# One decoding and prompt step of a hybrid network: the decays' exponents bounded on ScalarE instead of VectorE

## The chip, the cores and the metric

The kernel runs on 1 core of one Trainium2 chip. Its time is the device time of one execution in microseconds (us), the median of several runs. Engines are named as in the profile: PE (TensorE matmul), PEld (TensorE weight load), DVE (VectorE), ACT (ScalarE), POOL (GpSimd), SP (SyncE, which issues the DMAs here). Each engine works through its own list of instructions in order: an instruction that waits holds up all that stand behind it on that engine.

## What is computed

Two layers over 512 prompt tokens and 8 decode tokens, width 1024, all in float32. Layer 0 mixes with a gated DeltaNet (GDN, 8 heads), layer 1 with a Mamba-2 state space scan (SSD, 32 heads in 4 groups); after each mixer comes a LayerNorm, a gated convolutional feed-forward network and a second LayerNorm. The change touches one piece of each mixer, the decay matrix inside a chunk:

```python
gcum = jnp.cumsum(gc, axis=2)                       # GDN: running sum of the log decays, never rising
gamma = jnp.exp(jnp.where(incl, gcum_h[..., :, None] - gcum_h[..., None, :], -jnp.inf))
qk = jnp.einsum('bnihd,bnjhd->bnhij', qc, kc) * gamma
...
seg = jnp.exp(jnp.where(incl, acum_h[..., :, None] - acum_h[..., None, :], -jnp.inf))   # SSD
cb = jnp.einsum('bnigs,bnjgs->bngij', cc, bc)
scores = seg.reshape(...) * cb[:, :, :, None]       # one mask-and-decay product for each head
y_diag = jnp.einsum('bnghij,bnjghp->bnighp', scores, xg)
```

Where i is before j the difference is positive and its exponential could overflow. The kernel bounds the exponent at zero and masks the product afterwards (the mask is already in `CB`, and in GDN a later product with `U` does it).

## The kernel before

Tokens lie along the free axis in two halves of 260 columns, features on the 128 partitions, and a chunk is 128 tokens (C = 4 chunks). `plan` writes a list of units; one unit is one output tile of 128 rows of one weight matrix, for one or both halves of the tokens. `unit` (L225) issues, for each half and each 128 rows of the contraction, three matmuls (L243: high parts, and the two cross products of high and low parts of weights and x), so 24 matmuls for a half unit with a contraction of 1024. `prep` loads a unit's weights (512 KB), rounds them on ACT (L220) and makes the low part on DVE or POOL (L221). `unit_bank` gives the accumulators: two PSUM banks, and outside the GDN's scan a third. A bank is free again when ACT has copied it out, in GDN by L590 (`u<-psl`), in SSD by L425 and L439 (`u<-psl`) or by the gate's L1035 (`z<-psl`).

A tile `u` then goes through a short convolution (`conv`: one ACT instruction at L413, three DVE instructions at L416) and a Silu on ACT (L601 in GDN, L1052 in SSD).

The GDN layer asks for the decays of a head in `gdn_decays` (L727): one DMA spreads the head's running sums over all partitions (`gbc<-gd`), four DVE instructions add the column of the token j and bound at zero (L734, one for each chunk, 128x128), one ACT instruction takes the exponential of the whole tile (L736).

The SSD layer calls `ssd_group` for each of the 4 groups when the group's last x tile is through its convolution. After the product `CB` of C and B (L1143), the transposed x times dt (`xdt`, L1157) and the chunk states (matmul `sst` L1164; `Sn`, L1167 to L1170), it goes over 4 pairs of heads. Each head loads `E` by one DMA (`sE<-ad`, L1181), bounds it by four DVE instructions (L1183, in order `(E - a) min 0`), takes the exponential on ACT (L1185), multiplies by `CB` (L1187: on DVE for the second head of a pair, on POOL for the first), and PE uses it (`yd`, L1189). `yo` (L1193) brings in the states. The decode tokens' work (L1233 to L1246) and the D term (L1200) are on DVE beside it.

The code is written in the order of the computation, but the order on each engine is set by a scheduler that places every instruction by its own estimates of durations (`schedule_with_timeline_sim=True`); `high_priority()` marks what it should place early. A change in one instruction's engine can so move others anywhere in the program. ACT needs one table set for Exp, another for Silu and another for Sqrt; where neighbours on ACT differ, the compiler puts a table load (`ACT_TABLE_LOAD`) between them.

Of the kernel before, what the change touches and what calls it, by code (L numbers as in the profile page):

```python
# [13 lines left out]
ALU = mybir.AluOpType  # L14
# [8 lines left out]
B = 8  # L23
# [50 lines left out]
class Net:  # L74
# [39 lines left out]
    def unit_bank(self):  # L114
        """Two banks, and outside the GDN's scan a third."""
# [13 lines left out]
    def plan(self):  # L129
        """units: (name, m, halves, [(chunk, first block in it, first k, number of k)]) in order of use;  # L130
        chunks: (array, index, first block, number of blocks), the weights that are loaded together."""
# [42 lines left out]
    def _parts(self, name, nm, ka, kb, nfull):  # L174
        """Rows 0 .. nm first over k < ka (tag a), then over the rest (b), the other rows at once."""
# [25 lines left out]
    def lo_pool(self, i):  # L201
        """Whether the low parts of a unit's weights are made on GpSimd."""
        name, _, halves, _ = self.units[i]
        return name in ("gin", "sin") and len(halves) == 2 and (name == "gin" or i % 4 != 3)
# [20 lines left out]
    def unit(self, evac):  # L225
        """Runs the next unit; evac(name, m, half, psum)."""
# [66 lines left out]
    def ln_add(self, xr, out, m, h, ps):  # L293
        """The residual plus the first products."""
# [3 lines left out]
    def ln_evac(self, name, m, h, ps):  # L298
        """Rows of x, less the mean of the first NS of them."""
# [64 lines left out]
    def ln_half(self, h, row):  # L364
# [4 lines left out]
        # d = x - shift, whose sum over the first rows is 0: the variance is mean(d^2) - mean(d)^2  # L369
# [50 lines left out]
    def first_half(self, w, key, ps, keep):  # L420
        """The first half of a tile that a convolution takes: kept, or in DRAM until the second is there."""
# [89 lines left out]
    def softplus(self, pool, z, n, tag):  # L511
        """max(z, 0) + log1p(exp(-|z|)), the logarithm as 2 atanh(e / (2 + e))."""
# [17 lines left out]
    def rsqrt_small(self, pool, x, y, n, tag):  # L530
        """y = x ** -0.5 for a few columns: the exponent's half as the start, then Newton's steps."""
# [9 lines left out]
    def rsqrt(self, out, ps, eps):  # L541
        """out = (ps + eps) ** -0.5"""
# [5 lines left out]
    def tokens(self, pool, raw, name):  # L548
        """[64, T] -> [P, C + 1, 64], tokens on partitions; the last block holds the decode tokens."""
# [892 lines left out]
```

## Time and profile before

| | us |
|---|---|
| median of 3 runs | 1802.03 |
| lowest and highest run | 1801.03, 1809.23 |
| span of the profiled execution (first to last instruction) | 1799.5 |
| PE busy | 1613.9 (90%) |
| DVE busy | 1256.9 (70%) |
| POOL busy | 938.5 (52%) |
| ACT busy | 836.7 (46%) |

The page gives no other time for the profiled execution than its span. The span is 2.5 us under the median and 1.5 us under the lowest run; that much lies around the span. The shares are averages over stages that differ: the GDN's heads run from about 48 to 408 us, the SSD's groups from about 948 to 1228 us, and the feed-forward networks fill most of the rest. A PE that shows busy is not a PE at its peak, since matmuls are pipelined.

### The profile page before, as it was taken

How to read it: one execution, taken by the hardware profiler on the slowest of the kernel's cores; microseconds unless marked ns; L12 is line 12 of the kernel's file. 1: busy time of each engine (PE TensorE's matmuls, PEld its weight loads, DVE VectorE, ACT ScalarE, POOL GpSimd, SP SyncE). 2: the span in 40 equal slices, each digit the busy share in tenths (PEclk: the TensorE clock that was granted, in tenths of full speed). 3: DMA queues.
4: the chain of work that ended last, by engine and by line, in shares of the span. 5: the costliest groups of instructions: out<-in, count | busy, mean ns of one | idle time of the engine just before them, and what ended most of it. 6: DMA issues, size and time to landing. Idle time of an engine off the chain costs nothing.

```text
span 1799.5 us, 33950 instructions
## 1 busy us (share of the span) xinstructions
PE 1613.9 (90%) x12889; PEld 1550.6 (86%) x12889; DVE 1256.9 (70%) x2379; ACT 836.7 (46%) x1724; POOL 938.5 (52%) x1058
## 2 busy tenths in 40 slices
PE   7789888888899899999988888989989998899996
PEld 7788887788799899999887787879988998889996
DVE  5977897977876554336779988885659756554356
ACT  4554554335564344214665564645336633343134
POOL 4654555634538741225345757666224387876252
PEclk9999999899999999999999999999999999999998
DMA  5421333234466533334545434342464665664334
GB/s 181 135 84 60 95 112 104 86 110 155 135 200 213 177 121 97 88 98 122 163 148 172 150 124 140 118 136 65 146 197 150 203 205 174 196 213 153 95 101 143
DMA packets 108980, 250.38 MB, mean 139 GB/s; under 512 B 15344, under 2 KB 31696, under 8 KB 108784
## 3 DMA queue, kind: packets, MB, share of 16 engines
q1 hardware_dynamic: 108816, 248.20, 44.0%
q8 instruction: 101, 1.65, 0.4%
q14 instruction: 63, 0.52, 0.1%
HBM read 225.80 MB, written 22.92 MB: 138 GB/s over the span
## 4 chain that ended last, share of the span: by engine, by line
PE 32%; DVE 26%; DMA 17%; POOL 13%; ACT 6%; issue 5%; SPq 1%; ACTq 0%; DVEq 0%; POOLq 0%
PE psl L243 27%; DVE lo L221 4%; DMA Sr<-bd 3%; POOL Sd L993 3%; DMA raw<-w_up 3%; DVE sE L1183 3%; POOL Sr L991 2%; ACT hi L220 2%; DVE y L416 2%; POOL fl L276 2%; DMA raw<-w_down 2%; POOL Sd L992 2%; DMA Sr<-kr 2%; DMA Sd<-sstate 1%; DVE Xtmp L815 1%
## 5 line engine op out<-in xcount | busy, mean ns | idle before, releaser
L243 PE MATMUL psl<-XH,hi 128*128 128x260 f32 (+1 forms) x2816 | 818.9, 292 | 57.2 <-ACT u L439 18.7
L243 PE MATMUL psl<-XL,hi 128*128 128x260 f32 (+1 forms) x2848 | 823.4, 290 | 9.3 <-DVE lR L305 3.1
L243 PE MATMUL psl<-XH,lo 128*128 128x260 f32 (+1 forms) x2816 | 811.7, 289 | 4.3 <-DVE lo L221 3.9
L243 PEld LDWEIGHTS psl<-XH,hi 128*128 128x128 f32 (+1 forms) x2816 | 539.4, 192 | 72.7 <-ACT u L439 22.2
L221 DVE TENSOR_TENSOR lo<-raw,hi 128x512 fp32r<-128x512 f32 (+2 forms) x439 | 360.2, 856 | 321.4 <-ACT hi L220 313.7
L243 PEld LDWEIGHTS psl<-XL,hi 128*128 128x128 f32 (+1 forms) x2848 | 546.0, 192 | 16.6 <-issue 5.9
L243 PEld LDWEIGHTS psl<-XH,lo 128*128 128x128 f32 (+1 forms) x2816 | 539.5, 192 | 10.9 <-DVE lo L221 7.1
L220 ACT CAST hi<-raw 128x512 fp32r<-128x512 f32 (+2 forms) x499 | 314.2, 669 | 445.8 <-PE psl L243 209.0
L243 PE MATMUL psl<-fh,lo 128*128 128x260 f32 x704 | 201.5, 286 | 1.4 <-DVE lo L221 1.0
L243 PE MATMUL psl<-fh,hi 128*128 128x260 f32 x704 | 200.6, 285 | 0.0
L243 PE MATMUL psl<-fl,hi 128*128 128x260 f32 x704 | 199.0, 283 | 0.0
L221 POOL TENSOR_TENSOR lo<-raw,hi 128x1024 fp32r<-128x1024 f32 x60 | 147.5, 2458 | 62.2 <-ACT hi L220 60.7
L243 PEld LDWEIGHTS psl<-fh,lo 128*128 128x128 f32 x704 | 132.8, 189 | 3.3 <-DVE lo L221 3.0
L243 PEld LDWEIGHTS psl<-fh,hi 128*128 128x128 f32 x704 | 132.9, 189 | 0.5
L243 PEld LDWEIGHTS psl<-fl,hi 128*128 128x128 f32 x704 | 132.7, 189 | 0.3
L276 POOL TENSOR_TENSOR fl<-f,fh 128x260 fp32r<-128x260 f32 x88 | 79.9, 910 | 64.8 <-ACT fh L275 64.8
L416 DVE SCALAR_TENSOR_TENSOR s<-u,par,s 128x512 f32<-128x512 f32 x88 | 90.1, 1023 | 9.3 <-ACT s L413 8.1
L275 ACT CAST fh<-f 128x260 fp32r<-128x260 f32 x88 | 35.8, 407 | 91.3 <-DVE f L478 91.3
L243 PE MATMUL psl<-y,hi 128*128 128x260 f32 x256 | 73.3, 288 | 1.8 <-DVE y L276 0.8
L993 POOL TENSOR_TENSOR Sd<-Sd,Sr 128x512 f32<-128x512 f32 x48 | 69.4, 1445 | 0.6
L362 POOL TENSOR_TENSOR lnsq<-lnsq,sq 128x260 f32<-128x260 f32 x48 | 48.3, 1009 | 28.9 <-ACT sq L360 27.4
L1183 DVE TENSOR_SCALAR sE<-sE,acum 128x128 f32<-128x128 f32 x128 | 59.6, 525 | 3.0 <-DMA sE<-ad 2.9
(404 smaller groups left out, 2656.8 us busy)
## 6 DMA issues: line engine op xcount, KB each, us to landing
raw<-w_up SPq DMA_DIRECT2D x106, 512.0 KB
raw<-w_down SPq DMA_DIRECT2D x44, 512.0 KB
raw<-w_sin SPq DMA_DIRECT2D x43, 512.0 KB
raw<-w_gin SPq DMA_DIRECT2D x32, 512.0 KB
Sd<-sstate SPq DMA_DIRECT2D x64, 256.0 KB
raw<-w_down SPq DMA_DIRECT2D x22, 384.0 KB
Sd<-gstate SPq DMA_DIRECT2D x32, 256.0 KB
kb<-kr SPq DMA_DIRECT2D x32, 256.0 KB
```

The source lines that it names most:

```text
L220: nc.scalar.copy(out=hi[:, ks, :mw], in_=raw[:, ks, :])
L221: eng.tensor_tensor(out=lo[:, ks, :mw], in0=raw[:, ks, :], in1=hi[:, ks, :mw].bitcast(F32), op=ALU.subtract)
L243: self.nc.tensor.matmul(out=ps[h][:mw], lhsT=w[:, b0 + k, :mw], rhs=x[:, hs], start=(k0 + k == first and i == 0), stop=(k0 + k == last and ...
L275: nc.scalar.copy(out=hi, in_=xf)
L276: (eng or nc.gpsimd).tensor_tensor(out=lo, in0=xf, in1=hi.bitcast(F32), op=ALU.subtract)
L362: nc.gpsimd.tensor_tensor(out=acc, in0=acc, in1=sq, op=ALU.add)
L416: nc.vector.scalar_tensor_tensor(out=y[:, :S], in0=u[:, j:j + S], scalar=self.pcol(wname, i * w + j), in1=y[:, :S], op0=ALU.mult, op1=ALU.add)
L815: nc.vector.tensor_tensor(out=tmp[:, :, :, i:], in0=_bc(X16[:, None, :, i:], [P, 2, C, n]), in1=D[:, i:i + 2, :, i:], op=ALU.mult)
L991: nc.gpsimd.tensor_tensor(out=t, in0=t, in1=_bc(col[:, :, None], D4), op=ALU.mult)
L992: nc.gpsimd.tensor_tensor(out=St, in0=St, in1=_bc(decay[:, :, None], D4), op=ALU.mult)
L993: nc.gpsimd.tensor_tensor(out=St, in0=St, in1=t, op=ALU.add)
L1183: nc.vector.tensor_scalar(out=E[:, c, :], in0=E[:, c, :], scalar1=self.acum[:, c, h:h + 1], scalar2=0.0, op0=ALU.subtract, op1=ALU.min)
```

## The change

The bound becomes a rectifier on ACT, which takes the column of token j as its bias: `Relu(G_i' + G_j)` in GDN, where the loaded row is already negated, and `Relu(-E + a)` in SSD. The exponential that follows then has the scale -1. In SSD, the product with `CB` is on DVE for both heads of a pair. The diff also drops the comments and one line, so that line numbers behind L734 are smaller by one in the changed kernel, and by three behind L1187.

```diff
     def gdn_decays(self, p, h):
...
         for c in range(C):
-            nc.vector.tensor_scalar(out=gbc[:, c, :], in0=qe[:, c, :], scalar1=self.gcum[:, c, h:h + 1], scalar2=0.0,
-                                    op0=ALU.add, op1=ALU.max)
+            nc.scalar.activation(out=gbc[:, c, :], in_=qe[:, c, :], func=AF.Relu, bias=self.gcum[:, c, h:h + 1])
         nc.scalar.activation(out=both, in_=both, func=AF.Exp, scale=-1.0)
...
     def ssd_group(self, p, g, Bt, Ct):
...
                 for c in range(C):
-                    nc.vector.tensor_scalar(out=E[:, c, :], in0=E[:, c, :], scalar1=self.acum[:, c, h:h + 1], scalar2=0.0,
-                                            op0=ALU.subtract, op1=ALU.min)
-                nc.scalar.activation(out=E, in_=E, func=AF.Exp)
-                eng = nc.vector if s else nc.gpsimd
-                eng.tensor_tensor(out=E, in0=E, in1=CB, op=ALU.mult)
+                    nc.scalar.activation(out=E[:, c, :], in_=E[:, c, :], func=AF.Relu, scale=-1.0, bias=self.acum[:, c, h:h + 1])
+                nc.scalar.activation(out=E, in_=E, func=AF.Exp, scale=-1.0)
+                nc.vector.tensor_tensor(out=E, in0=E, in1=CB, op=ALU.mult)
```

The instructions counted: 32 in GDN (8 heads, 4 chunks) and 128 in SSD (32 heads, 4 chunks) go from DVE to ACT, and 16 products go from POOL to DVE. Over the whole program ACT has 70 table loads before and 72 after: 15 and 19 of them before the GDN layer's end, 43 and 41 among the SSD groups. None of the loads stands before a rectifier.

The order on the engines, at the places of which the prediction speaks. First DVE in the SSD layer, around the copy `Sn<-sst` that starts the states of the second group; `sE` is the decay tile, `dy` and `Sd` belong to the decode tokens. Before:

```order
L1241 TENSOR_REDUCE dy<-Sd 128x4
L1187 TENSOR_TENSOR sE<-sE,CB 128x512
L1246 SCALAR_TENSOR_TENSOR y<-y,par,dy 128x8
L221 TENSOR_TENSOR lo<-raw,hi 128x1024
L1183 TENSOR_SCALAR sE<-sE,acum 128x128 x8
L1170 COPY Sn<-sst 128x512
L1241 TENSOR_REDUCE dy<-Sd 128x4
```

And now:

```order
L1243 SCALAR_TENSOR_TENSOR y<-y,par,dy 128x8
L1184 TENSOR_TENSOR sE<-sE,CB 128x512
L1241 TENSOR_TENSOR dyt<-xdd,bcd 128x8
L1197 SCALAR_TENSOR_TENSOR y<-y,par,yd 128x512
L1184 TENSOR_TENSOR sE<-sE,CB 128x512
L1238 TENSOR_REDUCE dy<-Sd 128x4
L1169 COPY Sn<-sst 128x512
```

The eight bounds ahead of the copy are gone, and products with `CB` stand there.

Next ACT at the first SSD group, from the first bounds on; `u<-psl` are the copies that free a bank. Before, the stretch from the copy of the tile behind the group's C:

```order
L220 CAST hi<-raw 128x1024
L439 COPY u<-psl 128x260
L1185 ACTIVATE sE<-sE 128x512
L1148 COPY Bk<-bt 128x512
L413 ACTIVATE y<-u,par 128x520
L1185 ACTIVATE sE<-sE 128x512
L1052 ACT_TABLE_LOAD
L1052 ACTIVATE C<-C 128x520
L425 COPY u<-psl 128x260
```

And now:

```order
L1182 ACTIVATE sE<-sE,acum 128x128 x8
L1183 ACTIVATE sE<-sE 128x512
L220 CAST hi<-raw 128x1024
L439 COPY u<-psl 128x260
L1147 COPY Bk<-bt 128x512
L1183 ACTIVATE sE<-sE 128x512
L1182 ACTIVATE sE<-sE,acum 128x128 x4
L1051 ACT_TABLE_LOAD
L1051 ACTIVATE C<-C 128x520
L1182 ACTIVATE sE<-sE,acum 128x128 x4
L413 ACTIVATE y<-u,par 128x520
L425 COPY u<-psl 128x260
```

Eight rectifiers now stand ahead of the first of the two copies and eight more between them.

Last ACT at the start of the GDN's heads, from one copy `u<-psl` (L590) on. Before:

```order
L590 COPY u<-psl 128x260
L413 ACTIVATE kq<-u,par 128x520
L590 COPY u<-psl 128x260
L736 ACTIVATE gbc<-gbc 128x1024 x2
L220 CAST hi<-raw 128x1024
L590 COPY u<-psl 128x260
L601 ACT_TABLE_LOAD
L601 ACTIVATE kq<-kq 128x520 x2
L413 ACTIVATE kq<-u,par 128x520
L590 COPY u<-psl 128x260
```

And now:

```order
L734 ACTIVATE gbc<-gbc,gc 128x128 x8
L413 ACTIVATE kq<-u,par 128x520
L590 COPY u<-psl 128x260
L735 ACTIVATE gbc<-gbc 128x1024
L734 ACTIVATE gbc<-gbc,gc 128x128 x2
L601 ACT_TABLE_LOAD
L601 ACTIVATE kq<-kq 128x520
L734 ACTIVATE gbc<-gbc,gc 128x128 x2
L735 ACT_TABLE_LOAD
L735 ACTIVATE gbc<-gbc 128x1024
L734 ACTIVATE gbc<-gbc,gc 128x128 x4
L220 CAST hi<-raw 128x1024
```

The list goes on with a table load, `kq<-kq` and `v<-v` at L601, and only then the next copy `u<-psl`; a table load, the exponential at L735, another table load, `kq<-kq` and the copy after that follow. Before, two instructions of exponentials and one cast stand between the second copy and the third; now there are eight rectifiers, two exponentials, three table loads, three Silus and a cast.

## Rows read from the trace of the kernel before

**Rows 1.** The page's first part: each engine's busy time, its share of the span and its instructions.

```profile
PE 1613.9 (90%) x12889; PEld 1550.6 (86%) x12889; DVE 1256.9 (70%) x2379; ACT 836.7 (46%) x1724; POOL 938.5 (52%) x1058
```

**Rows 2.** Busy time of each engine by stretches of the span: the stretch in us, its length, then the busy us (and instructions) of PE, PEld, DVE, ACT and POOL, the granted TensorE clock as a share of the full 2.4 GHz, the DMA share and GB/s. The first stretch holds the GDN's heads, the second the SSD's groups, the others are parts of the second.

```profile
48.00:408.00 360.00, 305.31 (x2574) 290.12 (x2573) 303.01 (x845) 175.94 (x498) 192.43 (x228) 0.93 0.31 96
...
948.00:1228.00 280.00, 242.25 (x1820) 220.95 (x1820) 253.38 (x430) 152.90 (x217) 184.40 (x144) 0.95 0.43 134
960.00:1058.00 98.00, 80.50 (x593) 71.24 (x594) 92.71 (x178) 60.07 (x80) 64.13 (x53) 0.95 0.47 148
...
1100.00:1152.00 52.00, 46.12 (x328) 40.06 (x328) 45.60 (x83) 30.08 (x39) 39.73 (x31) 0.93 0.46 142
...
1196.00:1228.00 32.00, 27.01 (x187) 23.54 (x186) 27.36 (x51) 14.10 (x20) 22.84 (x18) 0.89 0.38 120
```

**Rows 3.** The chain of waits that ended last, within 948 to 1228 us, as shares of that stretch by engine and line.

```profile
by line: DVE sE L1183 16.4%; PE psl L243 9.9%; DVE y L416 8.6%; issue 5.3%; DMA sE<-ad 4.7%; DVE dy L1241 4.1%; DVE sE L1187 3.0%; DVE Sd L1240 2.6%; DVE y L1273 2.5%; DVE C L416 2.5%; PE yd L1189 2.5%; POOL sE L1187 2.0%; POOL lo L221 1.9%
```

**Rows 4.** For whom PE waited within 948 to 1228 us: waiting line, awaited line, us in total, times, longest.

```profile
PE yo L1193 <- DVE Sn L1170: 9.7, 2, 5.7
PE xtk L509 <- DVE xdt L1157: 7.9, 3, 2.9
```

**Rows 5.** Instructions in order of time on DVE and on PE within the SSD's groups: start, us, engine, line, operation, tiles, count; in brackets the idle time before and what ended it.

```profile
959.50 0.86 DVE L1183 TENSOR_SCALAR sE<-sE,acum 128x128 f32<-128x128 f32 x4
...
1007.80 5.25 DVE L1183 TENSOR_SCALAR sE<-sE,acum 128x128 f32<-128x128 f32 x4
...
1016.10 0.60 PE L1193 MATMUL yo<-C,Sn 128*128 128x128 f32 x3 [2.97 <-DVE ea L1201]
...
1036.71 3.47 DVE L1183 TENSOR_SCALAR sE<-sE,acum 128x128 f32<-128x128 f32 x8
...
1040.83 0.80 PE L1193 MATMUL yo<-C,Sn 128*128 128x128 f32 x2 [5.68 <-DVE Sn L1170]
...
1120.80 3.04 DVE L1183 TENSOR_SCALAR sE<-sE,acum 128x128 f32<-128x128 f32 x4
...
1127.57 1.19 PE L1164 MATMUL sst<-xd,Bk 128*128 128x512 f32 x1 [4.27 <-DVE y L1246]
...
1206.90 5.92 DVE L1183 TENSOR_SCALAR sE<-sE,acum 128x128 f32<-128x128 f32 x8
...
1214.79 0.80 PE L1193 MATMUL yo<-C,Sn 128*128 128x128 f32 x2 [4.05 <-DVE Sn L1170]
```

**Rows 6.** POOL's instructions in order of time, in the same columns, while the second run of rows 5 was on DVE.

```profile
1008.09 2.35 POOL L221 TENSOR_TENSOR lo<-raw,hi 128x1024 fp32r<-128x1024 f32 x1
1010.41 1.31 POOL L1038 TENSOR_TENSOR y<-y,z 128x520 f32<-128x520 f32 x1
```

**Rows 7.** Groups of instructions: line, engine, operation, tiles and shapes, count, busy us and mean ns of one, idle time before them. The first two rows are DVE within 948 to 1228 us, the third POOL over the whole span, the fourth DVE within 48 to 408 us.

```profile
L1183 DVE TENSOR_SCALAR sE<-sE,acum 128x128 f32<-128x128 f32 x128 | 59.6, 525 | 3.0 <-DMA sE<-ad 2.9
L1187 DVE TENSOR_TENSOR sE<-sE,CB 128x512 f32<-128x512 f32 x16 | 15.9, 1004 | 2.4 <-ACT sE L1185 2.4
...
L1187 POOL TENSOR_TENSOR sE<-sE,CB 128x512 f32<-128x512 f32 x16 | 24.3, 1526 | 14.0 <-ACT sE L1185 14.0
...
L734 DVE TENSOR_SCALAR gbc<-gbc,gc 128x128 f32<-128x128 f32 x32 | 11.6, 412 | 4.3 <-DMA gbc<-gd 4.3
```

**Rows 8.** Two rows on ACT instructions of the same size that take a column for each partition: the group of L753 over the whole span (busy us, mean ns of one), and two of it back to back in order of time.

```profile
L753 ACT ACTIVATE Kd<-kt,gdec 128x128 f32<-128x128 f32 x32 | 10.5, 395 | 0.0
...
66.72 0.63 ACT L753 ACTIVATE Kd<-kt,gdec 128x128 f32<-128x128 f32 x2
```

**Rows 9.** The bounds of SSD (L1183) by stretches: the stretch, its length, DVE's busy us on them and their count.

```profile
960.00:1058.00 98.00, 37.31 (x78) 0.95 0.47 148
1100.00:1152.00 52.00, 13.94 (x32) 0.93 0.46 142
1196.00:1228.00 32.00, 7.82 (x16) 0.89 0.38 120
```

**Rows 10.** The start of the GDN's heads in order of time: ACT, and one row each of DVE and PE.

```profile
46.91 0.36 ACT L590 COPY u<-psl 128x260 f32<-128x260 f32 x1
47.31 0.82 ACT L413 ACTIVATE kq<-u,par 128x520 f32<-128x520 f32 x1
48.04 0.36 ACT L590 COPY u<-psl 128x260 f32<-128x260 f32 x1
50.19 1.07 ACT L736 ACTIVATE gbc<-gbc 128x1024 f32<-128x1024 f32 x1 [1.79 <-DVE gbc L734]
...
53.34 1.03 ACT L220 CAST hi<-raw 128x1024 fp32r<-128x1024 f32 x1
54.27 0.37 ACT L590 COPY u<-psl 128x260 f32<-128x260 f32 x1
54.66 1.28 ACT L601 ACT_TABLE_LOAD   x1
55.95 1.17 ACT L601 ACTIVATE kq<-kq 128x520 f32<-128x520 f32 x2
...
57.74 0.35 ACT L590 COPY u<-psl 128x260 f32<-128x260 f32 x1
...
48.19 1.96 DVE L734 TENSOR_SCALAR gbc<-gbc,gc 128x128 f32<-128x128 f32 x4 [1.28 <-DMA gbc<-gd]
...
54.69 0.39 PE L243 MATMUL psl<-XH,hi 128*128 128x260 f32 x1 [1.36 <-ACT u L590]
```

## The prediction

> **What bounds the kernel now.** I read the page's first part, then the stretches, then in the stretch that the change touches the chain of waits, PE's waits, and last the instructions in order of time. Over the whole span PE is the busiest engine at 90%, DVE 70%, ACT 46% [rows 1]. That mean hides the SSD's groups, 948 to 1228 us: there DVE is busy 253.4 of 280 us and PE 242.3, and in 960 to 1058 us, where the bounds of two groups fall together, DVE is busy 92.7 of 98 us, PE 80.5 and ACT 60.1 [rows 2]. So in that stretch DVE sets the pace. The chain says the same: the bounds (L1183) hold 16.4% of it, 46 of 280 us, more than any other line [rows 3]. PE's longest waits there end with DVE [rows 4].
>
> In order of time one sees why. Four bounds take 0.86 us where nothing hinders them, and 5.25 us in another place; eight take 3.47 or 5.92 us [rows 5]. During the 5.25 us POOL ran one long elementwise instruction after the other [rows 6]. The mean bound takes 525 ns and all 128 hold DVE for 59.6 us [rows 7]; at the unhindered spacing, 0.86 / 4 = 0.215 us, they would take 27.5 us. More than half of their time is a stall. The Trainium skill ("SBUF — State Buffer", section "Who interferes with whom") says that DVE and GpSimd share a pair of ports, which one of them holds for a whole instruction, and that ACT never waits for it. The trace agrees as to DVE (0.86 against 5.25 us); that a rectifier on ACT stays free of it, no row here shows.
>
> **What goes from DVE in SSD.** All of the 59.6 us, and 16 more products with CB come: 16 x 1.004 = 16.1 us at the mean of those that DVE does now [rows 7]. Net 43.5 us less for DVE in the groups. POOL loses 24.3 us [rows 7], which was not what PE waited for. What of it lies on PE's path: four waits of PE stand directly behind a run of bounds, 2.97 (1016 us), 5.68 (1041 us), 4.27 (1128 us) and 4.05 us (1215 us) [rows 5]. That is 17.0 us, 8.65 of it in the first burst and 8.3 in the later two. I take these as what the change can give; PE's whole idle time there, 280 - 242.3 = 37.7 us [rows 2], is the upper end.
>
> **What comes to ACT.** No row shows a rectifier. The nearest are 128x128 instructions with a column for each partition, 395 ns alone, and 0.63 us for two back to back, so 0.24 us for each one that follows [rows 8]. Bounds: 0.24 and 0.395 us. The order has them in runs of 4 and 8, so I take 0.39 + 7 x 0.24 = 2.07 us for eight, 0.26 each. All 160 are then 41.6 us (38 to 63).
>
> 128 - 32 - 16 = 80 of the SSD's bounds fall in the first burst or just ahead of it [rows 9]. They put 80 x 0.26 = 20.8 us on top of ACT's 60.1 there: 81 of 98 us, 83%, more than ACT holds in any stretch now [rows 2]. On its in-order list the copies that free PE's banks stand behind runs of rectifiers (order of ACT at the first SSD group). Ten runs of eight could each hold a copy by 2.07 us, 20.7 us in all, or none, since PE has three banks there. I take 6 us, nearer to none. So the first burst gives 8.65 - 6 = 2.65 us.
>
> In the later bursts ACT is at 30.1 of 52 and 14.1 of 32 us [rows 2], with room for 32 x 0.26 = 8.3 and 16 x 0.26 = 4.2 us (counts of [rows 9]). The 8.3 us of waits go; but these 48 bounds belong to 6 pairs of heads, so 6 of POOL's products are now on DVE, 6 x 1.004 us, and I put half of them ahead of something that PE waits for (`xdt`, L1157 [rows 4]): 3 us. Together 8.3 - 3 = 5.3 us.
>
> SSD: -2.65 - 5.3 = **-8 us**.
>
> **GDN.** DVE loses 32 bounds, 11.6 us [rows 7], of 303.0 busy us in 360 [rows 2]. The danger is the start, where four heads' decays come at once. I walk ACT's list there (last order fence) with durations of [rows 8, 10]. The first copy ends at 47.27 us. The decays land at 48.19 (the DVE row waited for them until then). Eight rectifiers 2.07, the convolution's 0.73 (it overlaps its follower): the second copy starts at 51.0 instead of 48.04. Then 0.36 + exponential 1.07 + two rectifiers 0.63 + table load 1.28 + Silu 0.64 + two rectifiers 0.63 + table load 1.28 + exponential 1.07 + four rectifiers 1.11 + cast 1.03 + table load 1.28 + two Silus 1.17 = 11.55 us: the third copy at 62.6 instead of 54.27, **8.3 us later**. The fourth: 0.37 + 1.28 + 1.07 + 1.28 + 0.64 = 4.6, at 67.2 instead of 57.74, 9.5 us later. PE has only two banks in this stage and waited 1.36 us for the third copy already [rows 10]; it can't run ahead, and the first head's keys and queries pass through the same list. The four table loads that the order adds in GDN are all in this stretch and counted.
>
> What comes back: the 16 bounds of the later heads leave DVE, 16 x 0.215 (unhindered) to 16 x 0.412 us [rows 7], 3.4 to 6.6 us on an engine that is 84% busy; I take 4. GDN: +8.3 - 4 = **+4 us** (from -4, if the start is absorbed by waits that PE had anyway, to +13, if nothing comes back).
>
> **The sum.** -8 + 4 = -4 on a span of 1799.5, so 1795.5, and 2.5 us around it as the median of the runs has it: **1798 us**. A measurement of this kernel tells about 0.5% (9 us) from no change, so this forecast is "no difference", with a slight lean to faster.
>
> **Rivals.**
>
> *The DVE relief goes through to PE.* If ACT finds room between its waits, and PE gets back the 17.0 us of waits, the 7.9 us for `xdt` [rows 4], and with fewer gaps a granted clock nearer to 1.00 than the 0.95 of this stretch [rows 2] (at half of that, 242 x 0.025 = 6 us), SSD gives 31 us, less some 3 us for the products on DVE: 28. With GDN at +4: 1802 - 24 = **1778 us**. For it: the chain's 46 us and a DVE at 95% in the first burst. Against: ACT at 83% there.
>
> *ACT becomes what the stage waits for (slower).* With 0.395 us for each rectifier the first burst puts 80 x 0.395 = 31.6 us on ACT, 91.7 of 98 us, and ACT still has to wait for data. It decides from the point where ACT's list, work plus waits, is longer than the burst: ACT idles 38 of 98 us now, and if 18 of these remain, the burst takes 91.7 + 18 = 110 us, 12 more. The later bursts keep their 5 us gain, GDN has +13: 1802 + 12 - 5 + 13 = **1822 us**. The Trainium skill ("ScalarE: Activation LUTs", section "Rules for kernel authors") says to do relu, max and min on VectorE and not on ScalarE. By the unhindered row it is right for one instruction, 0.215 us against 0.26 to 0.395; by the mean of 0.525 us it is not. The rule leads to this rival.
>
> *Nothing moves.* Waits of PE go over to other late work of DVE and DMA, GDN's start is absorbed: 1802 us. It would lie with the forecast in the same verdict. That the change adds more table loads than counted (72 against 70 in all) is excluded by the order.
>
> **How the numbers follow.** Forecast (around 1798, own range 1790 to 1808) 0.43; relief passed on (1765 to 1790) 0.30; ACT the bound (1811 to 1826) 0.20; nothing moves 0.07. Faster by over 0.5% (below 1793): the second case and a part of the first, 0.36. Slower (above 1811): the third and a little, 0.21. Within: 0.43. The range from **1773 to 1822** leaves out about 2 in 10: the better half of the second case's lower part and the worst of the third.
>
> **What would show it.** In the changed profile: the bounds on ACT at 0.24 to 0.40 us each; DVE in the SSD's groups down from 253 to about 210 busy us, ACT up from 153 to about 186, PE's waits behind `Sn` (L1169 there) gone. The third copy `u<-psl` of [rows 10] at about 62 us, and PE idle before it by some 8 us with ACT as the releaser. In the first burst ACT above 80% and waits of PE for ACT's copies, which are absent there now. The prediction is wrong if the first SSD burst becomes shorter by more than 8 us, if PE doesn't wait at the GDN's start, or if ACT takes over the chain of the whole SSD stage.

## The result: 1821.2 us, 0.97% slower, and the profile after

The median is 1821.2 us (1816.56 to 1824.54, 5 runs) against 1802.03 us; the ratio is 1.0097, with a 95% interval from 1.0077 to 1.0117. The profiled execution has a span of 1821.0 us, 21.5 more than before. Four views tell where they went. First the page's busy times, which answer to [rows 1]:

```profile
PE 1631.9 (90%) x12889; PEld 1566.7 (86%) x12889; DVE 1206.8 (66%) x2235; ACT 888.0 (49%) x1886; POOL 912.2 (50%) x1042
```

DVE has 50 us less, ACT 51 more, as meant. But PE, whose work is the same to the instruction, is busy for 18 us longer.

Second, the stretches. They are cut at the same piece of work in both kernels: the first runs from half unit 9 of the projection matmuls (L243, 24 matmuls each) to half unit 96, which is the GDN heads and the LayerNorm behind them; the second runs from the first `cb` matmul of SSD to the last `yo`. Columns as in [rows 2]. Before:

```profile
40.38:513.56 473.18, 405.10 (x3341) 384.52 (x3339) 390.69 (x1019) 241.81 (x636) 237.68 (x287) 0.95 0.36 110
948.91:1241.73 292.82, 255.95 (x1932) 234.62 (x1933) 257.15 (x435) 156.47 (x224) 197.40 (x152) 0.95 0.43 133
```

With the change, and behind them three bursts that answer roughly, not instruction by instruction, to the last three of [rows 2]:

```profile
40.47:539.45 498.98, 422.39 (x3341) 400.56 (x3340) 383.73 (x987) 256.93 (x672) 237.60 (x286) 0.91 0.34 105
973.25:1257.74 284.49, 255.00 (x1911) 233.79 (x1912) 216.94 (x322) 191.71 (x349) 171.77 (x136) 0.96 0.43 137
975.00:1070.00 95.00, 84.02 (x601) 73.67 (x601) 79.96 (x128) 78.24 (x155) 52.59 (x46) 0.95 0.52 168
1115.00:1170.00 55.00, 48.00 (x366) 43.36 (x365) 39.27 (x58) 37.13 (x72) 39.32 (x29) 0.97 0.48 152
1212.00:1244.00 32.00, 26.20 (x173) 22.29 (x172) 29.16 (x41) 20.77 (x37) 24.93 (x18) 0.89 0.42 128
```

The SSD groups are 8.3 us shorter (292.82 to 284.49). Here they are cut once more, at the last `yd` matmul of the second group, two rows before and two with the change:

```profile
948.91:1050.87 101.96, 82.66 (x614) 73.44 (x614) 99.25 (x189) 61.80 (x82) 68.23 (x55) 0.95 0.48 152
1050.87:1241.73 190.86, 173.29 (x1319) 161.18 (x1319) 157.90 (x247) 94.67 (x144) 129.16 (x97) 0.96 0.40 122
...
973.25:1062.18 88.93, 77.95 (x554) 68.09 (x554) 77.98 (x127) 72.24 (x142) 52.02 (x44) 0.94 0.53 169
1062.18:1257.74 195.56, 177.04 (x1359) 165.71 (x1359) 138.96 (x195) 119.46 (x208) 119.76 (x92) 0.97 0.39 122
```

PE's idle time falls from 19.3 to 11.0 us in the first two groups, and rises from 17.6 to 18.5 in the last two. PE has 60 instructions fewer in the first part and 40 more in the second (some records are missing from a trace).

The GDN stretch is 25.8 us longer: PE's idle time grew from 68.1 to 76.6 us, 8.5, and its busy time from 405.1 to 422.4, 17.3, for the same 3341 instructions. The granted clock explains the latter in this pair: 405.1 x 0.95 / 0.91 = 422.9. But the split between waits and clock belongs to the pair. The kernels e2, e5, e6 and e15 below leave the GDN layer as it was, with the same order on PE, ACT, DVE and POOL, and their profiled executions, on several chips, show other splits of nearly the same length. Those of e5 and e15:

```profile
40.40:516.43 476.03, 413.42 (x3340) 393.70 (x3339) 390.61 (x1019) 241.85 (x636) 237.33 (x287) 0.92 0.36 110
...
40.09:511.84 471.75, 412.11 (x3340) 392.37 (x3339) 386.82 (x1019) 242.06 (x636) 239.30 (x287) 0.93 0.36 111
```

With one and the same order, PE is busy for 405.1 to 413.4 us and idle for 59.6 to 68.1, at a clock of 0.92 to 0.95, and the stretch takes 471.2 to 476.0 us. Against these five the change has 9.0 to 17.3 us more of busy PE and 8.5 to 17.0 more of idle PE: matmuls that ran slower are somewhere between a third and two thirds of the loss, and waits are the rest.

Outside the two stretches the profiled execution is 4.0 us longer, 5.5 of it more behind the SSD groups and 1.6 less between the stretches. Behind the groups the executions below spread over 10 us.

Third, in the SSD groups, for whom PE waited (columns as in [rows 4]) and what the moved instructions take:

```profile
PE yd L1186 <- DVE sE L1184: 7.0, 3, 5.1
PE xtk L509 <- DVE CB L1142: 3.6, 3, 2.3
PE yd L1186 <- DVE y L1197: 3.5, 2, 3.0
...
PE yd L1186 <- ACT sE L1182: 2.4, 1, 2.4
```

```profile
L1182 ACT ACTIVATE sE<-sE,acum 128x128 f32<-128x128 f32 x128 | 40.2, 392 | 28.7 <-DMA sE<-ad 26.1 <-DVE dy L1242 2.4
...
L1184 DVE TENSOR_TENSOR sE<-sE,CB 128x512 f32<-128x512 f32 x32 | 33.6, 1076 | 2.0 <-ACT sE L1183 1.9
...
996.50 2.46 ACT L1182 ACTIVATE sE<-sE,acum 128x128 f32<-128x128 f32 x8
```

PE's waits behind `Sn` and `xdt`, 17.6 us in [rows 4], are gone from the top of the list; the longest wait is now for the products with `CB`, 7.0 us. ACT sat idle for 26.1 us ahead of rectifiers whose `sE` had not landed; of PE's waits one, 2.4 us, ended with a rectifier.

Fourth, ACT at the start of the heads, in order of time, which answers to [rows 10]:

```profile
47.01 0.36 ACT L590 COPY u<-psl 128x260 f32<-128x260 f32 x1
48.74 1.29 ACT L734 ACTIVATE gbc<-gbc,gc 128x128 f32<-128x128 f32 x4 [1.37 <-DMA gbc<-gd]
50.40 1.28 ACT L734 ACTIVATE gbc<-gbc,gc 128x128 f32<-128x128 f32 x4 [0.36 <-DMA gbc<-gd]
51.58 0.81 ACT L413 ACTIVATE kq<-u,par 128x520 f32<-128x520 f32 x1
52.30 0.36 ACT L590 COPY u<-psl 128x260 f32<-128x260 f32 x1
...
63.60 0.35 ACT L590 COPY u<-psl 128x260 f32<-128x260 f32 x1
...
68.19 0.36 ACT L590 COPY u<-psl 128x260 f32<-128x260 f32 x1
```

and what PE did behind the second copy:

```profile
52.70 0.39 PE L243 MATMUL psl<-XH,hi 128*128 128x260 f32 x1 [2.15 <-ACT u L590]
52.93 0.28 PE L243 MATMUL psl<-XL,hi 128*128 128x260 f32 x1
53.05 0.36 PE L243 MATMUL psl<-XH,lo 128*128 128x260 f32 x1
53.21 0.42 PE L243 MATMUL psl<-XH,hi 128*128 128x260 f32 x1
53.42 0.42 PE L243 MATMUL psl<-XL,hi 128*128 128x260 f32 x1
...
63.22 1.12 PE L509 MATMUL kt<-cn,kq 128*128 128x128 f32 x4 [5.85 <-ACT kq L601]
```

The copies are about as late as forecast. PE waited 2.15 us, then worked at full clock for some tenths of a us, and from 53.21 us the same matmul takes 0.42 instead of 0.28 us: the clock has gone from the upper to the lower level. Then it waited 5.85 us for the first head's keys.

### The profile page after: what moved, and what is told of

Its sections match the earlier page's. It is cut to its first block, busy times and chain, and to the rows that moved or that the text cites. A ratio compares the mean times of both kernels' runs of the same rounds, so it can differ in the third digit from the quotient of the medians.

```text
span 1821.0 us, 33916 instructions
## 1 busy us (share of the span) xinstructions
PE 1631.9 (90%) x12889; PEld 1566.7 (86%) x12889; DVE 1206.8 (66%) x2235; ACT 888.0 (49%) x1886; POOL 912.2 (50%) x1042
## 4 chain that ended last, share of the span: by engine, by line
PE 28%; DVE 26%; DMA 18%; POOL 13%; ACT 9%; issue 5%; SPq 1%; ACTq 0%; POOLq 0%; DVEq 0%
PE psl L243 25%; DVE lo L221 3%; POOL Sd L992 3%; DMA Sr<-bd 3%; DMA raw<-w_up 3%; ACT hi L220 2%; POOL Sr L990 2%; POOL Sd L991 2%; DVE kq L416 2%; DMA Sd<-sstate 2%; DMA raw<-w_down 2%; DMA Sr<-kr 1%; POOL fl L276 1%; DVE y L416 1%; DMA sE<-ad 1%
## 5 line engine op out<-in xcount | busy, mean ns | idle before, releaser
L243 PE MATMUL psl<-XH,hi 128*128 128x260 f32 (+1 forms) x2816 | 826.4, 294 | 59.0 <-ACT u L439 20.0
L243 PE MATMUL psl<-XL,hi 128*128 128x260 f32 (+1 forms) x2848 | 829.0, 292 | 11.0 <-DVE lR L305 4.0
L243 PE MATMUL psl<-XH,lo 128*128 128x260 f32 (+1 forms) x2816 | 817.1, 291 | 6.1 <-DVE lo L221 5.1
L243 PEld LDWEIGHTS psl<-XH,hi 128*128 128x128 f32 (+1 forms) x2816 | 546.4, 194 | 74.8 <-ACT u L439 23.4
L243 PEld LDWEIGHTS psl<-XL,hi 128*128 128x128 f32 (+1 forms) x2848 | 551.6, 194 | 18.6 <-issue 5.9
L243 PEld LDWEIGHTS psl<-XH,lo 128*128 128x128 f32 (+1 forms) x2816 | 545.7, 194 | 12.0 <-DVE lo L221 8.1
L243 PE MATMUL psl<-fh,lo 128*128 128x260 f32 x704 | 201.1, 286 | 1.7 <-DVE lo L221 1.4
L243 PE MATMUL psl<-fh,hi 128*128 128x260 f32 x704 | 200.3, 285 | 0.6 <-ACT hi L220 0.6
L243 PE MATMUL psl<-fl,hi 128*128 128x260 f32 x704 | 198.8, 282 | 0.0
L243 PEld LDWEIGHTS psl<-fh,lo 128*128 128x128 f32 x704 | 132.5, 188 | 3.8 <-DVE lo L221 3.6
L243 PEld LDWEIGHTS psl<-fh,hi 128*128 128x128 f32 x704 | 132.5, 188 | 1.5 <-ACT hi L220 1.0
L243 PEld LDWEIGHTS psl<-fl,hi 128*128 128x128 f32 x704 | 132.4, 188 | 0.2
L276 POOL TENSOR_TENSOR fl<-f,fh 128x260 fp32r<-128x260 f32 x88 | 79.9, 910 | 64.3 <-ACT fh L275 64.3
L416 DVE SCALAR_TENSOR_TENSOR s<-u,par,s 128x512 f32<-128x512 f32 x88 | 82.8, 941 | 7.7 <-ACT s L413 6.7
L243 PE MATMUL psl<-y,hi 128*128 128x260 f32 x256 | 72.7, 285 | 1.8 <-DVE y L276 0.8
L954 POOL TENSOR_TENSOR kb<-kb,Sd 128x512 f32<-128x512 f32 x32 | 41.5, 1307 | 40.5 <-DMA kb<-kr 21.0
L468 POOL COPY cout<-u 128x10 f32<-128x10 f32 x44 | 20.8, 474 | 81.1 <-ACT u L439 81.1
```

What stands on the lines that cost most here:

```text
L243: self.nc.tensor.matmul(out=ps[h][:mw], lhsT=w[:, b0 + k, :mw], rhs=x[:, hs], start=(k0 + k == first and i == 0), stop=(k0 + k == last and ...
L276: (eng or nc.gpsimd).tensor_tensor(out=lo, in0=xf, in1=hi.bitcast(F32), op=ALU.subtract)
L416: nc.vector.scalar_tensor_tensor(out=y[:, :S], in0=u[:, j:j + S], scalar=self.pcol(wname, i * w + j), in1=y[:, :S], op0=ALU.mult, op1=ALU.add)
L468: nc.gpsimd.tensor_copy(out=cout[:, m, :], in_=u[:, 2 + S - 2:2 + T])
L954: nc.gpsimd.tensor_tensor(out=m, in0=m, in1=Sd, op=ALU.mult)
```

## The experiments

Ratios are to the kernel before, timed beside each, with the 95% interval. "GDN stretch" is the one from half unit 9 to 96 of the profiled execution, with its idle time of PE and granted clock. The last two columns are read from PE's instruction list, which is fixed when the program is built: how many half units stand ahead of the transposes `kt` of heads 0 to 4, and ahead of `ot` of head 0. The kernel before took 1802.0 to 1805.7 us beside these runs, so the ratios compare better than the times. A profiled execution is one of several: those of e16 and e20 were the fastest of their six, 8 and 6 us under the median.

| run | ratio (interval) | GDN stretch us, idle, clock | `kt` of heads 0 to 4 | `ot` |
|---|---|---|---|---|
| before | 1 | 473.2, 68.1, 0.95 | 14.0, 22.8, 29.8, 35.6, 39.8 | 41.5 |
| the change | 1.0097 (1.0077 to 1.0117) | 499.0, 76.6, 0.91 | 13.0, 21.0, 27.9, 33.7, 39.0 | 39.0 |
| e1 | 1.0146 (1.0121 to 1.0170) | 498.4, 78.4, 0.92 | as the change | 39.0 |
| e2 | 0.9960 (0.9944 to 0.9977) | 475.6, 68.1, 0.94 | as before | 41.5 |
| e5 | 0.9959 (0.9938 to 0.9979) | 476.0, 62.6, 0.92 | as before | 41.5 |
| e6 | 0.9999 (0.9984 to 1.0013) | 471.2, 64.5, 0.94 | as before | 41.5 |
| e15 | 1.0005 (0.9985 to 1.0025) | 471.8, 59.6, 0.93 | as before | 41.5 |
| e3 | 1.0029 (1.0011 to 1.0046) | 476.7, 68.2, 0.93 | as before | 41.4 |
| e4 | 1.0110 (1.0079 to 1.0140) | 493.0, 79.4, 0.92 | 13.0, 21.0, 27.9, 33.7, 38.6 | 39.4 |
| e10 | 1.0089 (1.0066 to 1.0111) | 484.2, 65.0, 0.92 | 13.9, 22.7, 29.5, 34.8, 39.5 | 40.3 |
| e11 | 0.9996 (0.9980 to 1.0012) | 471.5, 62.9, 0.94 | as before | 41.5 |
| e12 | 1.0021 (1.0000 to 1.0043) | 478.6, 69.0, 0.93 | 14.0, 23.0, 29.9, 35.7, 40.0 | 40.8 |
| e13 | 1.0019 (0.9999 to 1.0039) | 478.8, 70.4, 0.94 | 14.0, 23.0, 30.0, 35.7, 40.1 | 40.8 |
| e14 | 0.9961 (0.9942 to 0.9980) | 475.6, 66.3, 0.94 | as e12 | 40.8 |
| e16 | 1.0092 (1.0069 to 1.0115) | 484.6, 71.8, 0.93 | 14.0, 22.0, 30.0, 36.0, 40.5 | 42.0 |
| e17 | 1.0108 (1.0088 to 1.0128) | 490.1, 71.7, 0.91 | 14.0, 22.0, 28.0, 33.5, 37.7 | 40.8 |
| e18 | 1.0099 (1.0073 to 1.0124) | 495.1, 79.9, 0.91 | 14.0, 20.0, 26.0, 31.8, 36.0 | 38.9 |
| e19 | 0.9993 (0.9978 to 1.0009) | 480.7, 66.0, 0.93 | 16.0, 24.7, 32.0, 38.0, 44.0 | 43.0 |
| e20 | 1.0097 (1.0070 to 1.0124) | 484.4, 70.1, 0.92 | 14.0, 22.8, 30.0, 36.0, 40.5 | 41.3 |
| e21 | 1.0120 (1.0095 to 1.0145) | 491.9, 72.6, 0.91 | 14.0, 22.0, 30.0, 36.0, 40.5 | 42.0 |

### Which layer: e1, e2, and which heads: e3, e4

e1 takes the diff of L734 alone, e2 that of `ssd_group` alone. e3 and e4 make L734 a choice by head:

```diff
-            nc.vector.tensor_scalar(out=gbc[:, c, :], ...)
+            if h >= 4:          # e4: h < 4
+                nc.scalar.activation(out=gbc[:, c, :], in_=qe[:, c, :], func=AF.Relu, bias=self.gcum[:, c, h:h + 1])
+            else:
+                nc.vector.tensor_scalar(out=gbc[:, c, :], ...)
```

e1: 

> Only the GDN bounds (32) are rectifiers on ACT; the SSD layer is as in the kernel before. If the loss of the change sits in the GDN layer and the SSD part is a gain of its own (in the changed trace the program was 24.8 us late at the end of the GDN's work and 18 to 19 us late after the SSD groups): about 1802 + 25 = 1827 us. Rival, that ACT as the bound of the SSD groups makes the loss: about 1802 + 4 = 1806 us.

e2: 

> Only the SSD layer is changed (128 rectifiers on ACT, all products with CB on DVE); GDN is as in the kernel before. If the SSD part is a gain: about 1802 - 6 = 1796 us. Rival, ACT as the bound of the SSD groups: 1809 us or more. Rival, that the relief goes through to PE once the stage does not start late: about 1775 us.

e3: 

> In GDN the bounds of heads 4 to 7 are rectifiers on ACT, those of heads 0 to 3 stay on DVE; the SSD layer is as in the kernel before. If the loss comes from the jam on ACT at the start of the heads (16 rectifiers and 4 more table loads between 48 and 70 us): 1802 us or a little below (1796 to 1804), and the third copy u<-psl at about 54 us. Rival, that every rectifier on ACT costs the heads it serves the same: about 1802 + 12 = 1814 us.

e4: 

> In GDN the bounds of heads 0 to 3 are rectifiers on ACT, those of heads 4 to 7 stay on DVE; the SSD layer is as in the kernel before. If the loss comes from the jam at the start: about 1802 + 25 = 1827 us, with the third copy u<-psl at about 63 us. Rival, that every rectifier costs the same: about 1814 us. A third theory, that any other order of the scan moves the end of GDN by 10 to 20 us either way, whatever stands on ACT: this run and the one with heads 4 to 7 would not add up to that with all eight heads.

Measured: e1 1830.41 us, e2 1796.55 us (ratio 0.9960, 0.9944 to 0.9977), e3 1807.75 us, e4 1824.36 us. So the SSD part gains 7 us and the GDN part loses 26, of which the first four heads bring 20 and the last four 4 or 5. ACT does not bound the SSD groups. e3 moves just the sixteen bounds of the later heads, which the prediction counts as a gain of 4 us, and it loses 2 to 8 us by its interval. The parts of e3 and e4 add up to 24 of e1's 26 us, so by its own sign e4's third theory, that any other order of the scan moves the end of GDN, failed; e16 to e21 bring it back.

### What of SSD gains: e5, e6, e15

```diff
 e5: bounds on ACT, products as before
-                nc.vector.tensor_tensor(out=E, in0=E, in1=CB, op=ALU.mult)
+                eng = nc.vector if s else nc.gpsimd
+                eng.tensor_tensor(out=E, in0=E, in1=CB, op=ALU.mult)
 e6: the kernel before, with eng = nc.vector for both heads
 e15: as e5, with the rectifiers only for s == 1 (scale of Exp -1.0 if s else 1.0)
```

e5: 

> The SSD bounds are rectifiers on ACT, but the products with CB stay split between DVE and POOL as before; GDN as before. If the gain of the SSD part comes from the bounds leaving DVE, and the 16 products cost DVE about as much as PE gains by having them sooner: 1795 to 1800 us, the same as with all products on DVE (1796.6). Rival, that the products on DVE are what gains (POOL took 1.53 us for one, DVE 1.0): 1802 us or more. Rival, that they cost (half of 16 x 1.0 us): about 1789 us.

e6: 

> Only the products with CB move: all 32 on DVE; all bounds stay on DVE, GDN as before. If DVE sets the pace in the SSD's groups, 16 x 1.0 us more on it make it later: 1806 to 1815 us. Rival, that POOL's products were what stalled DVE's bounds, so that DVE gets back in stalls what it takes over: about 1802 us or below.

e15: 

> In the SSD layer only the bounds of the second head of each pair (64) are rectifiers on ACT, the first head's stay on DVE, the products stay split; GDN as before. If the gain of the SSD part goes with the bounds that leave DVE: half of it, about 1799 us. If ACT holds the stage back with all 128 on it (it sat idle for 27 us there ahead of rectifiers that waited for sE<-ad): below 1796 us, better than all.

Measured: e5 1796.75 us (0.9959, 0.9938 to 0.9979), e6 1804.86 us (0.9999, 0.9984 to 1.0013), e15 1806.88 us (1.0005, 0.9985 to 1.0025). The gain is all from the bounds; where the products run makes no difference that these intervals, some 4 us either way, can tell. Half of the bounds gave no gain, against both theories of e15 (half of the gain, a ratio of 0.998, lies just outside the interval). In e6, the bounds and the products on DVE in the SSD groups:

```profile
L1183 DVE TENSOR_SCALAR sE<-sE,acum 128x128 f32<-128x128 f32 x128 | 59.5, 525 | 5.6 <-DMA sE<-ad 5.6
...
L1187 DVE TENSOR_TENSOR sE<-sE,CB 128x512 f32<-128x512 f32 x32 | 31.7, 1014 | 0.2
```

and in e15 the half that stayed on DVE:

```profile
L1186 DVE TENSOR_SCALAR sE<-sE,acum 128x128 f32<-128x128 f32 x64 | 39.7, 675 | 8.0 <-DMA sE<-ad 8.0
```

With the products gone from POOL the bounds still take 525 ns each, as in [rows 7]; so it was not those products that stalled them. e6 put 15.8 us more on DVE (15.9 to 31.7) and lost nothing, although no stall came back: its first theory failed, and its rival gave the right time for a reason that did not come. DVE's busy time alone is thus not the measure of what the SSD groups wait for. With half of the bounds left, each takes 675 ns: 39.7 us of the 59.6 remain on DVE, and so DVE is relieved by a third, not by half. That goes some way to explain e15, but doesn't show why nothing at all was gained; this stays open.

### The place on ACT's list: e10, e11, e12 to e14

e10 and e11 are as e4 with `h < 2` and `h in (2, 3)`. e12 puts all 32 rectifiers on ACT, but queues those of heads 0 and 1 behind a copy that frees a bank, for which two more units are written ahead of the first head; e13 is that order of writing with the bounds on DVE, and e14 is e12 with the SSD part, so the whole change:

```diff
-                    nc.scalar.copy(out=u[...], in_=ps)
+                    st["copy"] = nc.scalar.copy(out=u[...], in_=ps)
...
-                e = self.gdn_decays(p, 0)
...
-                    for j in range(3):
+                    for j in range((5, 1)[h] if h < 2 else 3):
                         self.unit(evac)
-                    nxt = self.gdn_decays(p, h + 1) if h + 1 < H else None
+                    if h == 0:
+                        with self.tc.issue_after(st["copy"].ins):
+                            e = self.gdn_decays(p, 0)
+                            nxt = self.gdn_decays(p, 1)
+                    else:
+                        nxt = self.gdn_decays(p, h + 1) if h + 1 < H else None
```

e10: 

> In GDN the bounds of heads 0 and 1 alone are rectifiers on ACT, all others on DVE; the SSD layer as before. The ACT order has eight rectifiers ahead of the second copy u<-psl and two more table loads ahead of the third; the third copy should end at about 59 us instead of 54.3 (63.6 with four heads). If the delay of the third and fourth copy is what costs, about in proportion (20 us for 9.3 us of delay with heads 0 to 3): about 1802 + 12 = 1814 us. Rival, that the rectifiers count and not their place: half of 20, 1812 us here, and the same with heads 2 and 3 in their place.

e11: 

> In GDN the bounds of heads 2 and 3 alone are rectifiers on ACT; the SSD layer as before. The ACT order has the eight rectifiers between the second and the third copy u<-psl and no table load there; the third copy should come at about 57 us instead of 54.3. If the delay of the copies is what costs, in proportion: about 1802 + 6 = 1808 us, less than with heads 0 and 1. Rival, that the rectifiers count and not their place: 1812 us, as with heads 0 and 1.

e12: 

> All 32 GDN bounds are rectifiers on ACT, but those of heads 0 and 1 are queued behind the first half's copies of the next units (two more units are written ahead of the first head, and its decays issue only after the last of their copies that is known); the SSD layer as before. On ACT's list the second copy u<-psl has no rectifier ahead of it, the third has eight, and the table loads are the 74 of the kernel with all GDN bounds on ACT. If the second and third copy at the start are what costs (third copy at about 54.5 us as before, fourth at about 64.4): 1802 + 4 (heads 4 to 7) = 1806 us. Rival, that the number of rectifiers and table loads on ACT at the start costs, wherever they stand: about 1825 to 1830 us.

e13: 

> The same order of writing (two more units ahead of the first head, the first decays behind their copies) with all bounds on DVE as before: what that order does by itself. 1802 us if it does nothing; a difference of 10 us or more would say that the order of writing, and not where the bounds stand, moves the GDN layer.

e14: 

> The whole change (GDN and SSD) with the first two heads' decays held back behind the copies. If the two parts add up: 1806 - 8 = 1798 us, and 1821 - 1798 = 23 us of the change come back. Rival, that the loss stays: 1818 us or more.

Measured: e10 1821.46 us, e11 1802.50, e12 1808.64, e13 1808.58, e14 1798.52. The same eight rectifiers cost 17 us for heads 0 and 1 and nothing for heads 2 and 3: it is not their number. Both runs missed what their theories gave (1812 to 1814 and 1808 to 1812 us). In e10's profiled execution, 22 us longer than before, only 11.0 us lie in the GDN stretch and 7 lie behind the SSD groups; why is open. e12 has all 32 rectifiers and the 74 table loads of e1 and costs no more than e13, which has none of them on ACT; and e14, the whole change, is 0.4% faster than before, by the ratios 1.4% better than the change as it was.

At this point I held the late copies at the start for the cause. The trace of e12 spoke against it:

```profile
47.03 0.35 ACT L590 COPY u<-psl 128x260 f32<-128x260 f32 x1
51.57 0.70 ACT L738 ACTIVATE gbc<-gbc,gc 128x128 f32<-128x128 f32 x2 [4.18 <-DMA gbc<-gd]
...
56.81 0.37 ACT L590 COPY u<-psl 128x260 f32<-128x260 f32 x1
...
66.64 0.36 ACT L590 COPY u<-psl 128x260 f32<-128x260 f32 x1
```

The second copy was on time, but ACT waited 4.18 us for the decays; the third came at 56.81 us (54.27 before), the fourth at 66.64 (57.74 before, 68.19 with the change). At half unit 16 PE was 10.3 us late, with the change 10.6; yet at half unit 32 e12 was 0.8 us late, the change 14.0. A late start can be caught up. What differs is the order, which the table's last columns show on PE's list: with the change (and in e1 and e4; in e10 by 0.1 to 0.8) the work of heads 0 to 4 stands about 1 to 2 half units earlier among the projections, in e12 to e14 within 0.3 of where it stood before.

### PE's order by itself: e16 to e21

These hold places on PE's list by hand and leave the bounds where each run's text says; the scheduler places the rest anew around the pins, on the other engines too. In e16, e19, e20 and e21 the transposes `kt` of the first heads issue only behind a later unit, in e17 and e18 units issue only behind a head's `kt`:

```diff
 e16 (and e20 with L734 as before; e21 with h < 4 and units (6, 4, 4, 3, 0, 1, 3, 3)):
-                    for j in range(3):
+                    for j in range((6, 4, 4, 3, 2, 3, 2, 0)[h]):
...
-        for c in range(C):
-            self.transpose(kt[:, c, :], kq[:, 0, cs(c)])
+        pin = self.tc.issue_after(self.mm.ins) if h < 5 else contextlib.nullcontext()
+        with pin:
+            for c in range(C):
+                self.transpose(kt[:, c, :], kq[:, 0, cs(c)])
 e17 (and e18 with {9: 1, 12: 2, 15: 3, 18: 4, 21: 5}), in unit():
+                after = self.kts.get({10: 1, 13: 2, 16: 3, 19: 4, 21: 5}.get(m)) if name == "gin" else None
+                with self.tc.issue_after(after.ins) if after else contextlib.nullcontext():
                     for k in range(kn):
```

Here `self.mm` is the last matmul that was written and `self.kts[h]` the last transpose of head h. e19 has e2's SSD layer and units (7, 4, 4, 3, 3, 2, 1, 0).

e16: 

> All 32 GDN bounds are rectifiers on ACT, in the changed kernel's order on ACT at the start (eight ahead of the second copy u<-psl, all table loads), but the transposes kt of heads 0 to 4 are queued on PE behind 14, 22, 30, 36 and 40 half units (13, 21, 28, 34 and 39 with the change; 14, 23, 30, 36 and 40 before); the SSD layer as before. If PE's order makes the loss: 10 us late at unit 16 as with the change, but about 4 to 6 us at the end of GDN, 1806 to 1810 us. Rival, if the late copies at the start make it: 1826 to 1830 us.

e17: 

> All bounds on DVE, as in the kernel before; on PE some units are queued behind the heads' transposes kt, so that the heads stand earlier among the units (kt of heads 2 to 5 behind 28, 33.5, 37.7 and 43.1 half units instead of 29.8, 35.6, 39.8 and 45.6, the last xt behind 62.8 instead of 61.6). If PE's order makes the loss: 1810 to 1822 us with no lateness at unit 16. Rival, if the late copies make it: 1802 us.

e18: 

> As the run before, one unit further: kt of heads 1 to 5 behind 20, 26, 31.8, 36 and 41.4 half units, earlier than in the change. If PE's order makes the loss: 1815 to 1830 us, more than the run before. Rival, if the late copies make it: 1802 us.

e19: 

> The SSD part of the change, GDN's bounds on DVE, and the heads later on PE than before (kt behind 16, 25, 32, 38 and 44 half units instead of 14, 23, 30, 36 and 40). If later heads go on gaining by having more units ahead of them: below 1796 us. If the order before was near the best: 1797 to 1805 us.

e20: 

> All bounds on DVE, ACT's list at the start as before (second copy at about 48 us), and the pins of e16 on the transposes kt of heads 0 to 4; the later heads stand on PE as in e16 (kt behind 40.5, 46.0, 51.6 and 55.8 half units). If the order of the later heads makes the loss of e16: about 1815 to 1820 us. If the late copies make it: 1802 us.

e21: 

> As e16 (all 32 GDN bounds on ACT, the late copies at the start), with the pins on heads 0 to 3 only; the last heads stand nearer to the order before (kt of heads 5 to 7 behind 45.9, 51.2 and 55.4 half units, last wt 64.9 as before). If the order makes the loss, less than e16: 1806 to 1812 us. If the late copies make it: as e16, 1820 to 1824 us.

Measured: e16 1823.06 us, e17 1823.99, e18 1824.28, e19 1803.70 (0.9993, 0.9978 to 1.0009), e20 1819.86, e21 1825.56. In e17 and e18 every bound is on DVE and ACT's list at the start is the old one, with PE on time at half unit 16 (0.7 and 0.2 us early), and they lose as much as the change. So the loss needs no bound on ACT and no late start: another order is enough. Which engine's order it takes is not shown, since the lists of ACT, DVE and POOL in this stretch differ from before's too. e18, one unit further, did not lose more than e17, as it was expected to. The GDN stretch of e17, in the columns of [rows 2]:

```profile
39.70:529.79 490.09, 418.41 (x3341) 396.70 (x3339) 394.91 (x1019) 242.36 (x636) 234.86 (x286) 0.91 0.34 106
```

It is 16.9 us longer than before with the same work, 13.3 of it PE busy at a clock of 0.91 instead of 0.95 (against e5, with before's order at 0.92, it is 14.1 longer, and 5.0 of it PE busy). e14's, with all the rectifiers on ACT, is 2.4 us longer:

```profile
41.19:516.77 475.58, 409.27 (x3340) 388.03 (x3339) 386.01 (x987) 257.65 (x671) 238.15 (x286) 0.94 0.36 110
```

e16 was to be the counter-proof and looks at first like a failure: late copies, PE's order near the old one, and still 0.9% lost. Its control e20 says why. With the same pins, all bounds on DVE and no late copies it loses the same (1.0097 against 1.0092): the pins moved the heads from the fourth on (40.5 half units ahead of `kt` of head 4 instead of 39.8), and with that order come 17 us of loss. The late copies add nothing that can be measured, with each of the two ratios known to some 5 us. e21 missed: I had called its order nearer to the old one, and it lost more. e19, with every head about 2 to 4 half units later, loses 6 us against e2 (0.9993 against 0.9960). So what makes one order better than another I can't say from the half units ahead of `kt`; orders that moved some of heads 0 to 4 by 0.7 or more, in either direction, lost 6 to 26 us, those that kept them within 0.3 lost 5 at most.

## Why the prediction was wrong, point by point

- **SSD, -8 us: the sum right, by luck; its terms wrong.** The stretch is 8.3 us shorter, and the SSD part alone gains 7 us (e2). In the whole stretch DVE's busy time fell by 40.2 us (43.5 forecast) and ACT's rose by 35.2 (33.3 forecast); ACT is busy for 78.2 of 95 us in the first burst, 82% (83% forecast). PE's waits behind `Sn` fell from 9.7 us to 0.4. A rectifier takes 0.31 us in runs of eight (2.46 / 8) and 0.39 alone, against 0.26 and 0.395. But the first burst was to give 2.65 us and the later ones 5.3. In the first two groups PE's idle time fell by 8.3 us (19.3 to 11.0): the 6 us that I let ACT cost did not show. In the last two it rose by 0.9 (17.6 to 18.5): the waits behind the bounds went, and others came, the longest 5.1 us for a product with `CB`. The profiles of e2 and e14 show the same (idle 9.8 and 11.4 us in the first two groups, 18.5 and 18.7 in the last two). Two errors of some 6 us cancel. The first two groups are 13.0 us shorter (101.96 to 88.93, with 60 PE instructions fewer between the cuts); by that measure the prediction's first sign of being wrong came.
- **ACT's list at GDN's start, +8.3 us: the delay right, its price wrong.** Third copy at 63.60 us (62.6 forecast), fourth at 68.19 (67.2), PE 10.6 us late at half unit 16, and its waits there are for ACT's copies and for `kq`. As a cost it is not borne out: e12 is as late there (10.3 us) and takes the time of e13, which has no bound on ACT and no such delay.
- **The GDN term, +8.3 - 4 = +4 us: the step that failed.** I charged the late copies at their full length, counted the relief of DVE as the rest of the stage, and had no term for the new order that the scheduler gives the whole stage. In its place the GDN part lost 26 us (e1). The delay costs next to nothing by itself (e12 against e13, e16 against e20). The relief did not come: e3, with those sixteen bounds alone, lost 2 to 8 us. An order with the heads elsewhere on PE's list costs 17 to 20 us with every bound on DVE (e17, e18, e20), and all the rectifiers with an order near the old one cost next to nothing (e12, e14). I compared ACT's list and not PE's, where it stood to be read: `kt` of head 1 behind 21.0 half units instead of 22.8. The range for GDN, -4 to +13, had no room for it, and its upper end doesn't follow from the prediction's own numbers either: with nothing coming back they give +8.3 to +9.5.
- **The rival of ACT as the bound** gave 1822 us, the time that was measured, for a wrong reason: it has 7 us of loss in SSD, which gained 8.3, and 13 in GDN, which lost 25.8. A rival that gives the right number is not shown by it. By the rule of the Trainium skill ("ScalarE: Activation LUTs", section "Rules for kernel authors") the rectifiers should have been the loss; e14, with all 160 of them on ACT, is 0.4% faster, so here the measurement decides against it; in GDN, where e12 and e13 take the same time, the place of the bounds makes no difference that was measured.
- **The rival of the relief passing to PE** did not come: PE's idle time in the SSD stretch went from 36.9 to 29.5 us, and its clock from 0.95 to 0.96.

Open is what in the order costs the time. The sum of the waits does not tell: e17 has nearly before's share of idle time (71.7 of 490 us against 68.1 of 473, both 15% or just under) and still loses. The clock of one execution does not tell either: with before's order it was 0.92 to 0.95, and with the orders that lost 16 us or more 0.91 to 0.93. No run has the changed kernel's own order on all engines with the bounds on DVE; that orders cost this much is shown, that this one costs all of the 26 us is concluded from the runs around it.

## What to carry to other kernels

Where a scheduler sets the order from its own estimates, a change of an engine is two changes: the instruction's cost, and a new order on all engines. Compare the list of the engine that bounds the stage through the whole stage, not only at the place of the edit, and test the two apart: the old engines with the new order, and the new engines with the old order. If the gain is real and the order the loss, hold the old order, or leave out the part that upsets it: here e14 turned a ratio of 1.0097 into 0.9961, and leaving the GDN layer as it was (e2) gave 0.9960. That e14 found a good order is partly luck: it was meant to bring the copies in time, which came late all the same. And one profile against one profile does not tell waits from clock: take several of the same program first.

## What the runs showed of the hardware that I had not expected

- A rectifier on ACT took 384 to 407 ns by itself in every place of the SSD groups, all 128 of them. The same bound on DVE took 267 ns at the least and 2450 at the most; its mean was 525, and 675 with half of them left. Taking 16 products of 1.5 us off POOL (e6) did not change the 525. The columns are least, median and greatest ns, first and last start in us, and shapes:

```profile
L1182 ACT ACTIVATE sE<-sE,acum x128: 384/390/407, 982.1 to 1226.7; 128x128 f32<-128x128 f32 x128
...
L1183 DVE TENSOR_SCALAR sE<-sE,acum x128: 267/277/2450, 959.5 to 1212.5; 128x128 f32<-128x128 f32 x128
```

- Over the GDN stretch the same PE instructions, in the same order on all engines, were busy for 405.1 us at a clock of 0.95 in one execution and for 413.4 us at 0.92 in another, and the stretch was only 2.9 us longer (473.2 and 476.0), since PE waited less. The granted clock of one execution is no property of the program alone.
